# A decoder layer whose residual turns token-major, and whose MLP goes by slabs with seven half-size products

## The chip, the cores and the metric

The kernel runs on one core of a Trainium2 chip. Its engines work side by side, each through its own queue in order: TensorE multiplies matrices into PSUM banks, VectorE and ScalarE work element by element, GpSimd does a little of that too, and SyncE issues the DMAs that bring the weights. The metric is the device time of one launch in microseconds (us), the median of several runs.

## The reference

One decoder layer on 256 tokens, all in float32, with a residual stream of 2048 features, an MLP of 8192 hidden features and a per-layer embedding of 256:

```python
h = rmsnorm(x)
qA, kA, vA, qB, kB, vB, gA, gB = split(h @ w_in)
yA = dilated_mixture(qA, kA, vA)
yB = stick_breaking(qB, kB, vB)
x += (sigmoid(gA) * (yA @ w_branch_a) + sigmoid(gB) * (yB @ w_branch_b)) @ w_out
x += relu(rmsnorm(x) @ w_up) ** 2 @ w_down
x += (p @ w_ple_proj) * sigmoid(rmsnorm(x) @ w_ple_gate)
```

The change concerns what stands from `w_out` on: w_out is 2048x2048, w_up 2048x8192, w_down 8192x2048, w_ple_gate 2048x2048, w_ple_proj 256x2048.

## The kernel before, in words

**Two parts for each number.** TensorE's fast format (float32r) doesn't hold all of a float32. `split` makes of each operand a high part, a copy by ScalarE rounded to that format, and a low part, what is left, by VectorE. A product is then three: high by high, high by low and low by high. Activations have their two parts side by side in one tile (`[P, 4, 2, T]`: k tile, part, token). Weights come in chunks of 1 MB by SyncE (`load`, tiles `raw`), and each half chunk, 128 partitions by 1024 columns, is split into `wh` (ScalarE, L79) and `wl` (VectorE, L80). The pool `wts` has three buffers for each of raw, wh and wl; a buffer is free again when the matmuls that read it are done.

**Two shapes of product.** `group_t` gives feature-major results, 128 features on the partitions: the weight is the stationary operand, and for each k tile and each of two blocks of 128 features one matmul of 512 columns (L135: `wh` against the activation's both parts) and one of 256 (L136: `wl` against the high part) run. `halves` adds the two halves of the result. A chunk is eight k tiles of 256 weight columns, so 16 such pairs. `group_m` gives token-major results, 128 tokens on the partitions: the activation is stationary, and for each k tile and each block of 128 tokens three matmuls of 512 weight columns run (L150 to L152). Before the change only queries, keys and values use it, from `w_out` on all is feature-major.

**From w_out on.** `residual` adds each block of w_out's result to `x`, splits it times the gain as `h2`, and GpSimd collects the squares in `acc`; one matmul with ones (L178) sums these over the partitions. The norm comes in behind the product of up, as `rb` in L504. The MLP goes by four quarters of the hidden features: eight groups of up, whose results go through relu, square and split into `u`, then eight groups of down, each added to `x` by `residual`. The embedding's product is spread over the last quarter. The gate's groups end in `gate_out`.

**What sets the order.** Each engine's queue has the order that the framework's scheduler makes of the program text. `later` puts attention work, norms and embedding aside, and `advance` emits each when products of a given time have been emitted. PSUM has eight banks, four for the tag `mm` and four for `at`.

## Time and profile before

| | |
|---|---|
| median of 3 runs | 1494.01 us (1493.19 to 1505.6) |
| span of the profiled execution | 1494.2 us |
| mean granted TensorE clock | 0.998 of full |
| TensorE busy | 1480.9 us |
| VectorE busy | 1007.3 us |
| ScalarE busy | 783.1 us |
| moved by DMA | 277.10 MB |

The profile is one execution as the hardware recorded it. The span runs from its first instruction to its last, and no other time of that execution is given. Busy time is the time in which an engine had an instruction at work; TensorE's matmuls overlap, so how many it can do in a stretch is read from start to start. The granted clock is the share of full clock that the chip let TensorE have.

### The profile page before, as it was taken

What the parts mean: (1) busy time and instruction counts of PE and PEld (TensorE: products, weight loads), DVE (VectorE), ACT (ScalarE), POOL (GpSimd) and SP (SyncE); (2) the same over time, 40 slices, a digit from 0 to 9 for tenths busy, and PEclk for the clock granted to TensorE, in tenths of its full rate; (3) what the DMA queues carried; (4) which work ended last, traced back from release to release, by engine and by line L of the source; (5) the groups of instructions that cost most, each with busy time, mean ns of one, the idle gap of its engine ahead of it and who ended that gap; (6) DMA issues with size and microseconds to landing.
All of it is one profiled execution on the core that took longest, in us unless ns stands there. A gap on an engine that the chain in (4) does not pass through costs nothing.

```text
span 1494.2 us, 20920 instructions
## 1 busy us (share of the span) xinstructions
PE 1480.9 (99%) x8252; PEld 1285.3 (86%) x8252; DVE 1007.3 (67%) x1463; ACT 783.1 (52%) x1130; POOL 133.7 (9%) x137
## 2 busy tenths in 40 slices
PE   8999999999999999999999999999999999999998
PEld 6788888888888888888888888888888888888887
DVE  7875666466676667767766567656676567777776
ACT  6454554489845555555544445444454445555553
POOL 3432000000000000441000000000000000024200
PEclk9999999999999999999999999999999999999999
DMA  7455444544455555555555555555555555555563
GB/s 297 150 193 190 173 157 163 191 170 168 153 193 197 174 193 188 179 197 175 193 197 187 184 194 197 184 185 196 194 182 189 197 179 187 198 177 189 189 211 109
DMA packets 41281, 277.10 MB, mean 185 GB/s; under 512 B 4704, under 2 KB 7136, under 8 KB 8288
## 3 DMA queue, kind: packets, MB, share of 16 engines
q1 hardware_dynamic: 41040, 275.76, 52.3%
q8 instruction: 64, 1.05, 0.3%
q14 instruction: 33, 0.27, 0.1%
q10 hardware_dynamic: 144, 0.02, 0.0%
HBM read 273.67 MB, written 2.10 MB: 185 GB/s over the span
## 4 chain that ended last, share of the span: by engine, by line
PE 96%; DVE 2%; DMA 0%; ACT 0%; POOL 0%; issue 0%; SPq 0%; ACTq 0%; DVEq 0%; POOLq 0%
PE ps_mm L135 55%; PE ps_mm L136 28%; PE ps_mm L151 3%; PE ps_mm L152 3%; PE ps_mm L150 3%; DVE wl L80 1%; PE ps_at L135 0%; DMA x<-in_xt 0%; PE ps_at L319 0%; DVE h L83 0%; PE ps_mm L537 0%; PE ps_mm L539 0%; PE ps_mm L538 0%; PE ps_at L136 0%; PE ps_at L320 0%
## 5 line engine op out<-in xcount | busy, mean ns | idle before, releaser
L80 DVE TENSOR_TENSOR wl<-raw,wh 128x1024 fp32r<-128x1024 f32 (+1 forms) x518 | 636.2, 1229 | 361.6 <-ACT wh L79 355.2
L79 ACT ACTIVATE wh<-raw 128x1024 fp32r<-128x1024 f32 (+1 forms) x518 | 546.1, 1055 | 461.4 <-PE ps_mm L135 369.8
L135 PE MATMUL ps_mm<-h,wh 128*128 128x512 f32 x2016 | 712.3, 397 | 0.0
L136 PE MATMUL ps_mm<-h,wl 128*128 128x256 f32 x2016 | 564.7, 280 | 0.0
L135 PEld LDWEIGHTS ps_mm<-h,wh 128*128 128x128 f32 x2016 | 377.8, 187 | 87.0 <-ACT wh L79 0.3
L136 PEld LDWEIGHTS ps_mm<-h,wl 128*128 128x128 f32 x2016 | 380.8, 189 | 0.5
L135 PE MATMUL ps_mm<-u,wh 128*128 128x512 f32 x1024 | 356.9, 393 | 0.0
L136 PE MATMUL ps_mm<-u,wl 128*128 128x256 f32 x1024 | 286.9, 280 | 0.0
L135 PEld LDWEIGHTS ps_mm<-u,wh 128*128 128x128 f32 x1024 | 191.7, 187 | 43.6
L136 PEld LDWEIGHTS ps_mm<-u,wl 128*128 128x128 f32 x1024 | 193.5, 189 | 0.0
L161 ACT ACTIVATE ev<-ps_mm 128x256 f32<-128x256 f32 x158 | 59.7, 378 | 91.9 <-PE ps_mm L136 91.9
L150 PE MATMUL ps_mm<-wh,h 128*128 128x512 f32 x256 | 101.7, 400 | 2.6 <-ACT wh L79 2.6
L151 PE MATMUL ps_mm<-wl,h 128*128 128x512 f32 x256 | 101.5, 397 | 2.0 <-DVE wl L80 1.9
L454 POOL TENSOR_TENSOR acc<-x 128x256 f32<-128x256 f32 x2 | 3.3, 1653 | 1112.9 <-DVE x L449 1112.9
L152 PE MATMUL ps_mm<-wh,h 128*128 128x512 f32 x256 | 101.4, 396 | 0.0
L162 DVE TENSOR_TENSOR es<-ps_mm,ev 128x256 f32<-128x256 f32 x158 | 66.4, 421 | 44.2 <-ACT ev L161 44.0
L135 PE MATMUL ps_mm<-m,wh 128*128 128x512 f32 x256 | 90.5, 399 | 0.0
L136 PE MATMUL ps_mm<-m,wl 128*128 128x256 f32 x256 | 71.9, 281 | 0.0
L150 PEld LDWEIGHTS ps_mm<-wh,h 128*128 128x128 f32 x256 | 49.0, 192 | 14.8 <-ACT wh L79 4.9
L447 ACT ACTIVATE ev<-ps_mm 128x256 f32<-128x256 f32 x80 | 30.3, 379 | 59.0 <-PE ps_mm L136 59.0
L151 PEld LDWEIGHTS ps_mm<-wl,h 128*128 128x128 f32 x256 | 49.0, 191 | 13.8 <-DVE wl L80 3.8
L135 PEld LDWEIGHTS ps_mm<-m,wh 128*128 128x128 f32 x256 | 48.1, 188 | 12.1
(159 smaller groups left out, 1181.9 us busy)
## 6 DMA issues: line engine op xcount, KB each, us to landing
raw<-in_wup SPq DMA_DIRECT2D x64, 1024.0 KB, 4.7
raw<-in_wdn SPq DMA_DIRECT2D x64, 1024.0 KB, 4.8
raw<-in_wb SPq DMA_DIRECT2D x48, 1024.0 KB, 4.8
raw<-in_wa SPq DMA_DIRECT2D x31, 1024.0 KB, 4.8
raw<-in_wo SPq DMA_DIRECT2D x16, 1024.0 KB, 4.7
raw<-in_wpg SPq DMA_DIRECT2D x16, 1024.0 KB, 4.8
raw<-in_wba SPq DMA_DIRECT2D x8, 1024.0 KB, 4.7
raw<-in_wbb SPq DMA_DIRECT2D x8, 1024.0 KB, 4.7
```

The lines of the kernel that those rows point to most:

```text
L79: nc.scalar.activation(hi, src, AF.Copy)
L80: nc.vector.tensor_tensor(lo, src, hi.bitcast(F32), op=ALU.subtract)
L135: nc.tensor.matmul(ps[j], wh[:, c], flat(rhs[kt]), start=kt == 0, stop=False)
L136: nc.tensor.matmul(ps[j][:, :T], wl[:, c], rhs[kt][:, 0, :], start=False, stop=kt == last)
L150: nc.tensor.matmul(ps[tt], lhs[kt][:, 0, t], wh, start=kt == 0, stop=False)
L151: nc.tensor.matmul(ps[tt], lhs[kt][:, 0, t], wl, start=False, stop=False)
L152: nc.tensor.matmul(ps[tt], lhs[kt][:, 1, t], wh, start=False, stop=kt == last)
L161: nc.scalar.activation(t, ps[:, T:], AF.Copy)
L162: nc.vector.tensor_tensor(s, ps[:, :T], t, op=ALU.add)
L447: nc.scalar.activation(t, ps[:, T:], AF.Copy)
L454: nc.gpsimd.tensor_tensor(acc, xs(k), xs(k), op=ALU.mult)
```

## The change

Up to the end of the branches' merge (`m`) nothing changes but the pools. From `w_out` on:

- The residual stream is held token-major in two tiles `xr0` and `xr1` (128 tokens by 2048 features), loaded from a second copy of x, `xm`, 2 MB. w_out, w_down, the embedding and the gate become token-major products in the manner of `group_m`, and `add_rows` adds a bank of 512 columns to `xr`.
- The norm's squares are summed by ScalarE along each row (`squares_rows`), since a token is now a partition; `rows_norm` makes the reciprocal root. `turn` brings each finished piece of 512 columns feature-major, by transposes on TensorE into banks of the tag `at`, and splits it from there as h2 or h3.
- The norm before up isn't applied to up's result; its square, `r2`, scales down's result in `add_rows`.
- The MLP goes by eight slabs of 1024 hidden features. Slab 0's up stands alone; then `together` takes units of slab s's down and of slab s+1's up in turn. A unit of up is half a chunk (eight pairs), a unit of down a half chunk in `plain_units` (12 matmuls) or a whole product in `fast_units` (12 matmuls).
- For slabs 0 to 6, down's output columns 0 to 1023 are made by `fast_units`: the product of a 2x2 arrangement (two blocks of 128 tokens by two halves of 512 hidden features; these by two halves of 512 columns) in seven products of half size, not eight, 84 matmuls instead of 96. For it `hidden` makes four more planes by additions (tile `hr`), and the four quarters of the weight (tiles `quart`, 1 MB each) are added in place on VectorE. `keep` copies a bank between products (tile `cp`).
- Pools: `blk` has 6 buffers and `mblk` 9 in place of 15, `W1` is 7 instead of 8, and after w_out the mixers' pools are closed and `hid`, `mw` and `ps2` opened in their place. `ps2` has one bank each for x, z, w and y, two for `mm`, two for `at`.

The core of the diff:

```diff
+    def turn(g, h, gain, bank):
+        for half in range(2):
+            tp = bank("at")
+            for i in range(2):
+                k = 4 * g + 2 * half + i
+                for tt in range(2):
+                    o = (2 * i + tt) * P
+                    nc.tensor.transpose(tp[:, o:o + P], xr[tt][:, k * P:(k + 1) * P], ident)
+            for i in range(2):
+                k = 4 * g + 2 * half + i
+                split(h[k][:, 0, :], h[k][:, 1, :], tp[:, i * T:(i + 1) * T], gn[:, gain, k:k + 1])
...
+    for g in range(4):
+        ps = group_m([wo[g, c] for c in range(4)], m)
+        for tt in range(2):
+            add_rows(tt, g * PIECE, ps[tt])
+            squares_rows(tt, g, ss1, work.tile([P, PIECE], F32, tag="w2", name="junk", bufs=W2))
+        later(3, turn, g, h2, 1, bank)
...
+    def hidden(ps, fast):
+        n = 8 if fast else 4
+        s = mw.tile([P, 2, T], F32, tag="hs", name="hs", bufs=2)
         for j in range(2):
+            t = mw.tile([P, T], F32, tag="ev", name="ev", bufs=2)
+            nc.scalar.activation(t, ps[j][:, T:], AF.Copy)
+            nc.vector.tensor_tensor(s[:, j, :], ps[j][:, :T], t, op=ALU.add)
+        nc.scalar.activation(s, s, AF.Relu)
+        r = mw.tile([P, n, P], F32, tag="hr", name="hr", bufs=1)
+        nc.scalar.activation(r[:, 0:4, :].rearrange("p a t -> p (a t)"),
+                             s.rearrange("p a t -> p (a t)"), AF.Square)
+        if fast:
+            a21, a11, a22, a12 = (r[:, i, :] for i in range(4))
+            nc.vector.tensor_tensor(r[:, 4, :], a11, a21, op=ALU.subtract)
...
+        u = hid.tile([P, 2, n, P], F32R, tag="hid", name="u")
+        split(u[:, 0], u[:, 1], r)
+        return u
...
+    def up_units(s, out):
+        for g in range(4):
+            ps = [bank2("mm", 2) for _ in range(2)]
+            for c in range(2):
+                parts = weights(wup[4 * s + g, c], 8, 256)
...
+            out.append(hidden(ps, (s, 0) in FAST or (s, 1) in FAST))
+            yield
...
+        def product(ps, a, b, start):
+            for p0 in range(2):
+                for i, (wh, wl) in enumerate(split_weights(b[:, 2 * p0:2 * p0 + 2, :], 2, PIECE)):
+                    k = 2 * p0 + i
+                    nc.tensor.matmul(ps, f[k][:, 0, a, :], wh, start=start and k == 0, stop=False,
+                                     skip_group_check=not start)
+                    nc.tensor.matmul(ps, f[k][:, 0, a, :], wl, start=False, stop=False,
+                                     skip_group_check=not start)
+                    nc.tensor.matmul(ps, f[k][:, 1, a, :], wh, start=False, stop=k == 3,
+                                     skip_group_check=not start)
...
+        def add(a, b):
+            nc.vector.tensor_tensor(a, a, b, op=ALU.add)
...
+        product(px, A11, b[0, 0], True)
+        s1 = keep(px, 1)
+        add(b[0, 0], b[0, 1])
+        yield
+        product(pz, S1, b[0, 0], True)
+        z0 = keep(pz, 0)
+        add(b[0, 0], b[1, 1])
+        yield
+        product(px, S2, b[0, 0], False)
+        s2 = keep(px, 1)
+        add(b[0, 0], b[1, 0])
+        yield
+        product(pw, A22, b[0, 0], True)
+        w0 = keep(pw, 0)
+        add(b[0, 1], b[1, 1])
+        yield
+        product(py, A12, b[1, 0], True)
+        add(xr[1][:, left[0]], s1)
+        add_rows(1, c1, py, r2[:, 1:2])
+        yield
+        product(px, S3, b[0, 1], False)
...
+        product(pz, S4, b[1, 1], False)
```

The seven products are called P1 to P7 in this order below.

On VectorE, in the middle of a feature-major stage of the MLP before, the queue holds splits of weights (`wl`), the evacuation of up (`es`, `r2`) and its split (`u`):

```order
L80 TENSOR_TENSOR wl_7824<-raw_7821,wh_7823 128x1024
L80 TENSOR_TENSOR wl_7828<-raw_7821,wh_7827 128x1024
L162 TENSOR_TENSOR es_7802<-ps_mm_7715,ev_7801 128x256
L504 TENSOR_TENSOR es_7802<-es_7802,rb1_6193 128x256
L506 SCALAR_TENSOR_TENSOR r2_7806<-es_7802 128x256
L80 TENSOR_TENSOR wl_7866<-raw_7863,wh_7865 128x1024
L80 TENSOR_TENSOR u1_0_7711<-r2_7806,u1_0_7711 128x256
L162 TENSOR_TENSOR es_7811<-ps_mm_7716,ev_7810 128x256
L504 TENSOR_TENSOR es_7811<-es_7811,rb1_6193 128x256
```

On VectorE after the change, from the first split of P1's weight (`wl_7119`) of one slab on; `raw` belongs to up, `quart` to down, `hr` and `u` to the hidden features, L595 is `add`:

```order
L83 TENSOR_TENSOR wl_7129<-quart_7106,wh_7128 128x1024
L595 TENSOR_TENSOR quart_7106<-quart_7106,quart_7108 128x2048
L535 TENSOR_TENSOR hs_7089<-ps_mm_6955,ev_7090 128x256
L535 TENSOR_TENSOR hs_7089<-ps_mm_6956,ev_7093 128x256
L83 TENSOR_TENSOR wl_7146<-raw_7143,wh_7145 128x1024
L83 TENSOR_TENSOR wl_7150<-raw_7143,wh_7149 128x1024
L542 TENSOR_TENSOR hr_7097<-hr_7097 128x128
L543 TENSOR_TENSOR hr_7097<-hr_7097 128x128
L595 TENSOR_TENSOR quart_7108<-quart_7108,quart_7110 128x2048
L544 TENSOR_TENSOR hr_7097<-hr_7097 128x128
L83 TENSOR_TENSOR wl_7186<-quart_7106,wh_7185 128x1024
L545 TENSOR_TENSOR hr_7097<-hr_7097 128x128
```

The additions of weight quarters stand between the splits of up (`wl_7146`, `wl_7150`) and those of the next product (`wl_7186`). Some rows on it goes on so, to the last split of P7's weight, `wl_7440`:

```order
L83 TENSOR_TENSOR wl_7196<-quart_7106,wh_7195 128x1024
L83 TENSOR_TENSOR u_7103<-hr_7097,u_7103 128x1024
L595 TENSOR_TENSOR quart_7106<-quart_7106,quart_7110 128x2048
L83 TENSOR_TENSOR wl_7211<-raw_7208,wh_7210 128x1024
L83 TENSOR_TENSOR wl_7215<-raw_7208,wh_7214 128x1024
L83 TENSOR_TENSOR wl_7235<-quart_7106,wh_7234 128x1024
L595 TENSOR_TENSOR xr1_5282<-xr1_5282,cp_7138 128x512
L595 TENSOR_TENSOR xr0_5281<-xr0_5281,cp_7205 128x512
L83 TENSOR_TENSOR wl_7245<-quart_7106,wh_7244 128x1024
L595 TENSOR_TENSOR quart_7106<-quart_7106,quart_7112 128x2048
```

The split of the hidden block `u_7103` and that of the next up half chunk, `wl_7211`, each stand behind an addition of 128x2048.

On TensorE at the joint of w_out and the MLP before, the norm's product (L178) stands among up's pairs, some way into the first group:

```order
L135 MATMUL ps_mm<-h_3_5279,wh 128x512
L136 MATMUL ps_mm<-h_3_5279,wl 128x256
L178 MATMUL ps_at<-acc,cs 128x256
L135 MATMUL ps_mm<-h_3_5279,wh 128x512
L136 MATMUL ps_mm<-h_3_5279,wl 128x256
L135 MATMUL ps_mm<-h_3_5279,wh 128x512
```

On TensorE at the same joint after the change, from w_out's last matmuls (L153 to L155) over the last `turn` (L476) to up's first pair:

```order
L154 MATMUL ps_mm_5759<-wl_5887,m3_4000 128x512
L155 MATMUL ps_mm_5759<-wh_5886,m3_4000 128x512
L476 MATMUL ps_at_5920<-idt_82,xr0_5281 128x128
L476 MATMUL ps_at_5929<-idt_82,xr0_5281 128x128
L476 MATMUL ps_at_5920<-idt_82,xr1_5282 128x128
L476 MATMUL ps_at_5920<-idt_82,xr0_5281 128x128
L476 MATMUL ps_at_5920<-idt_82,xr1_5282 128x128
L476 MATMUL ps_at_5929<-idt_82,xr1_5282 128x128
L476 MATMUL ps_at_5929<-idt_82,xr0_5281 128x128
L476 MATMUL ps_at_5929<-idt_82,xr1_5282 128x128
L562 MATMUL ps_mm_5966<-h2_0_5285,wh_5970 128x512
L563 MATMUL ps_mm_5966<-h2_0_5285,wl_5971 128x256
```

The transposes of w_out's last piece now stand between w_out and up, where before no instruction of TensorE needed that piece for long.

## Rows read from the trace of the kernel before

**Rows 1.** Page: busy time of two engines; the chain that ended last, by engine.

```profile
PE 1480.9 (99%) x8252; PEld 1285.3 (86%) x8252; DVE 1007.3 (67%) x1463; ACT 783.1 (52%) x1130; POOL 133.7 (9%) x137
PE 96%; DVE 2%; DMA 0%; ACT 0%; POOL 0%; issue 0%; SPq 0%; ACTq 0%; DVEq 0%; POOLq 0%
```

**Rows 2.** Page, costliest groups: busy and mean ns, idle before and its releaser.

```profile
L80 DVE TENSOR_TENSOR wl<-raw,wh 128x1024 fp32r<-128x1024 f32 (+1 forms) x518 | 636.2, 1229 | 361.6 <-ACT wh L79 355.2
L79 ACT ACTIVATE wh<-raw 128x1024 fp32r<-128x1024 f32 (+1 forms) x518 | 546.1, 1055 | 461.4 <-PE ps_mm L135 369.8
```

**Rows 3.** Waits of TensorE: us in total, times, longest.

```profile
PE ps_at L288 <- POOL qn L282: 2.6, 1, 2.6
PE ps_mm L150 <- ACT wh L79: 2.6, 2, 1.5
PE ps_mm L151 <- DVE wl L80: 1.9, 2, 1.4
...
```

**Rows 4.** Timeline of TensorE, 900 to 908 us: start, duration, instruction.

```profile
900.18 0.39 PE L135 MATMUL ps_mm<-h,wh 128*128 128x512 f32 x1
...
907.46 0.39 PE L135 MATMUL ps_mm<-h,wh 128*128 128x512 f32 x1
```

**Rows 5.** Timeline of TensorE, 85 to 90 us, token-major.

```profile
86.23 0.40 PE L151 MATMUL ps_mm<-wl,h 128*128 128x512 f32 x1
...
89.86 0.39 PE L152 MATMUL ps_mm<-wh,h 128*128 128x512 f32 x1
```

**Rows 6.** Chain of waits in order of time: start, duration, transposes and norm product.

```profile
85.28 0.87 PE ps_at L288 x8
...
683.41 0.43 PE ps_at L178 x2
```

**Rows 7.** Groups by line and shape, whole kernel: busy, mean ns, idle before.

```profile
L162 DVE TENSOR_TENSOR es<-ps_mm,ev 128x256 f32<-128x256 f32 x158 | 66.4, 421 | 44.2 <-ACT ev L161 44.0
L161 ACT ACTIVATE ev<-ps_mm 128x256 f32<-128x256 f32 x158 | 59.7, 378 | 91.9 <-PE ps_mm L136 91.9
...
L83 DVE SCALAR_TENSOR_TENSOR h<-x,gn,h 128x256 fp32r<-128x256 f32 x48 | 37.0, 787 | 2.5 <-ACT h L82 2.4
...
L82 ACT ACTIVATE h<-x,gn 128x256 fp32r<-128x256 f32 x48 | 23.3, 506 | 2.4 <-DMA gn<-in_gains 0.8 <-DMA x<-in_xt 0.4
...
L360 ACT ACT_TABLE_LOAD x8 | 10.3, 1283 | 0.1
...
L273 DVE TENSOR_TENSOR qn<-qraw,qr 128x512 f32<-128x512 f32 x8 | 5.5, 693 | 0.4
...
L265 ACT ACTIVATE qraw<-ps_mm,rt 128x512 f32<-128x512 f32 x8 | 5.4, 676 | 3.1 <-PE ps_mm L152 3.1
...
L239 ACT ACTIVATE q<-x 128x512 f32<-128x512 f32 x8 | 4.6, 615 | 0.0
...
L335 ACT ACTIVATION_READ_ACCUMULATOR e<-z,st 128x1 f32 x16 | 3.0, 187 | 0.0
```

**Rows 8.** Windows: busy of PE, PEld, DVE, ACT, POOL; granted clock; DMA share; GB/s.

```profile
23.00:25.00 2.00, 2.00 (x10) 1.59 (x10) 2.00 (x2) 0.58 (x1) 1.87 (x2) 1.00 0.32 135
...
63.00:64.00 1.00, 1.00 (x4) 0.73 (x3) 0.87 (x4) 0.00 (x0) 0.00 (x0) 0.50 0.00 0
```

**Rows 9.** Timeline of TensorE at the two waits; idle time before in brackets.

```profile
22.73 0.50 PE L151 MATMUL ps_mm<-wl,h 128*128 128x512 f32 x1 [1.38 <-DVE wl L80]
...
61.20 0.66 PE L288 MATMUL ps_at<-cs,qn 128*128 128x128 f32 x4 [2.63 <-POOL qn L282]
```

**Rows 10.** Timeline of VectorE, 900 to 903 us: a split and the next instruction.

```profile
900.97 1.22 DVE L80 TENSOR_TENSOR wl<-raw,wh 128x1024 fp32r<-128x1024 f32 x1
902.11 0.42 DVE L80 TENSOR_TENSOR u<-r,u 128x256 fp32r<-128x256 f32 x1
```

**Rows 11.** Timeline of the end: the first and the last step behind the last product.

```profile
1489.68 0.42 DVE L522 TENSOR_TENSOR g<-ps_mm,rb 128x256 f32<-128x256 f32 x1 [0.42 <-PE ps_mm L539]
...
1491.11 0.42 DVE L525 TENSOR_TENSOR o<-o,x 128x256 f32<-128x256 f32 x1
```

More of the change, by code (lines that the diff above doesn't have):

```diff
@@ L183, in norm_rows @@
         return rb
-    x = [block([P, 8, T], F32, f"x{i}") for i in range(2)]
+    x = [block([P, 8, T], F32, f"x{i}", blk) for i in range(2)]
     gn = const.tile([P, 3, DT], F32, name="gn")
@@ L532, in layer_kernel @@
-    parts = [weights(wpg[7, c], 8, 256) for c in range(2)]
-    for j in range(2):
-        ps = bank("mm")[:, :T]
-        c = slice(j * P, (j + 1) * P)
-        for kt, (wh, wl) in enumerate(parts[0] + parts[1]):
-            nc.tensor.matmul(ps, wh[:, c], h3[kt][:, 0, :], start=kt == 0, stop=False)
-            nc.tensor.matmul(ps, wh[:, c], h3[kt][:, 1, :], start=False, stop=False)
-            nc.tensor.matmul(ps, wl[:, c], h3[kt][:, 0, :], start=False, stop=kt == DT - 1)
-        gate_out(14 + j, ps)
+    xr = [block([P, D], F32, f"xr{tt}", blk) for tt in range(2)]
@@ new lines, in layer_kernel @@
+    h2 = new_acts("h2_", pool=blk)
+    ss1 = const.tile([P, 2, 4], F32, name="ss1")
+    for g in range(4):
+        ps = group_m([wo[g, c] for c in range(4)], m)
+        for tt in range(2):
+            add_rows(tt, g * PIECE, ps[tt])
+            squares_rows(tt, g, ss1, work.tile([P, PIECE], F32, tag="w2", name="junk", bufs=W2))
+        later(3, turn, g, h2, 1, bank)
+    rms = []
+    later(6, lambda: rms.append(rows_norm(ss1, "rt1", work)))
+    advance(0)
+    while pending:
+        advance(1.0)
@@ new lines, in layer_kernel, with bank2 @@
+    mixers.close()
+    mlp = ExitStack()
+    hid = mlp.enter_context(tc.tile_pool(name="hid", bufs=7))
+    mw = mlp.enter_context(tc.tile_pool(name="mw", bufs=2))
+    ps2 = mlp.enter_context(tc.tile_pool(name="ps2", bufs=1, space=PSUM))
+    FAST = [(s, 0) for s in range(7)]
+    def bank2(tag, bufs=1):
+        return ps2.tile([P, 512], F32, tag=tag, name=f"ps_{tag}", bufs=bufs)
+    r2 = const.tile([P, 2], F32, name="r2")
+    r2n = const.tile([P, 1], F32, name="r2n")
+    nc.vector.tensor_tensor(r2, rms[0], rms[0], op=ALU.mult)
@@ new lines, in plain_units @@
+    def plain_units(s, n, u):
+        for j in range(2):
+            ps = [bank2("x" if tt else "z") for tt in range(2)]
+            for i in range(2):
+                raw = load(wdn[s, n, i, j], 4, PIECE)
+                for k, (wh, wl) in enumerate(split_weights(raw, 4, PIECE)):
+                    for tt in range(2):
+                        a = 2 * i + tt
+                        last = i == 1 and k == 3
+                        nc.tensor.matmul(ps[tt], u[k][:, 0, a, :], wh, start=i + k == 0, stop=False)
+                        nc.tensor.matmul(ps[tt], u[k][:, 0, a, :], wl, start=False, stop=False)
+                        nc.tensor.matmul(ps[tt], u[k][:, 1, a, :], wh, start=False, stop=last)
+                    advance(1.36)
+                    if k == 1:
+                        yield
+                if i == 0:
+                    yield
+            for tt in range(2):
+                add_rows(tt, (2 * n + j) * PIECE, ps[tt], r2[:, tt:tt + 1])
+            yield
@@ new lines, in down_units, with together @@
+    def down_units(s, u, done=None):
+        for n in range(2):
+            if (s, n) in FAST:
+                yield from fast_units(s, n, u)
+            else:
+                yield from plain_units(s, n, u)
+            if done is not None:
+                done(2 * n)
+                done(2 * n + 1)
+    def together(a, na, b, nb):
+        ia = ib = 0
+        for _ in range(na + nb):
+            if ia * nb <= ib * na and ia < na or ib >= nb:
+                next(a, None)
+                ia += 1
+            else:
+                next(b, None)
+                ib += 1
+        for x_ in (a, b):
+            for _ in x_:
+                pass
@@ new lines, in layer_kernel, with finished @@
+    ss2 = const.tile([P, 2, 4], F32, name="ss2")
+    h3 = []
+    def finished(g):
+        if g == 0:
+            h3.extend(new_acts("h3_", pool=blk))
+        for tt in range(2):
+            squares_rows(tt, g, ss2, mw.tile([P, PIECE], F32, tag="cp", name="junk", bufs=5))
+        later(3, turn, g, h3, 2, lambda tag: bank2("at", 2))
+    hids = [[]]
+    for _ in up_units(0, hids[0]):
+        pass
+    for s in range(8):
+        hids.append([])
+        if s < 7:
+            b, nb = up_units(s + 1, hids[s + 1]), 16
+        else:
+            b, nb = embedding_units(), 4
+        na = sum(7 if (s, n) in FAST else 8 for n in range(2))
+        together(down_units(s, hids[s], finished if s == 7 else None), na, b, nb)
@@ L593 @@
             for n, a in arrays.items()]
[L594 removed]
+    out = nc.dram_tensor("out", (2, P, D), F32, kind="ExternalOutput").ap()
     with tile.TileContext(nc) as tc:
```

229 lines of the change are left out of this document (138 added, 91 removed).

## The prediction, as it was written before the result

> **What bounds the kernel now.** I read the page's busy times and its chain first: TensorE is busy 99% of 1494.2 us, the chain of work that ended last is 96% TensorE and 2% VectorE, VectorE is busy 67% [rows 1]. So a product that is left out is worth its slot, as long as the next operand is there. Then the two rows of the split of a weight, which show who waits for whom: ScalarE makes `wh` and is idle 461 us, mostly for TensorE to free a buffer; VectorE makes `wl` and is idle 362 us, nearly all of it for `wh` [rows 2]. The splits run ahead as far as three buffers allow and then wait; TensorE waits for a split for only 2.6 and 1.9 us in the whole kernel [rows 3]. That lead over TensorE is the cover on which the change leans, so the question is what VectorE has left in each stage, not its 67%.
>
> The execution that was profiled has a span of 1494.2 us; the median of the three runs is 1494.01, so I sum against 1494.2. A measurement of this kernel tells about 1% (15 us) from no change.
>
> **What leaves TensorE and what comes.** A feature-major pair (512 and 256 columns) takes 0.3466 us from start to start (900.18 to 907.46 is 21 pairs) [rows 4]; a token-major matmul of 512 columns takes 0.227 (86.23 to 89.86 is 16) [rows 5]. Three of these do the work of two pairs: 0.681 against 0.693. w_down: 1024 pairs, 354.9 us, become 7 x (84 + 96) + 192 = 1452 matmuls, 329.6 us: -25.3. w_out: 256 pairs (88.7) become 384 matmuls (87.2): -1.5. The gate: 224 pairs and the last group's products (77.6 + 11.5) become 87.2: -1.9. Embedding -0.2. The two norm products of the kernel before (0.43 each, about 0.5 with their slot) go: -1.1. 64 transposes come at 0.11 (eight in 0.87 us) [rows 6]: +7.0. **Sum -23.0 us.** Up is unchanged. The 2 MB of `xm` and the embedding's other layout cost TensorE nothing: the loads that hide them have landed long before.
>
> **The joint between w_out and the MLP.** Before, `residual` turns out h2 feature by feature and the first up product needs only its k tile 0, long done. After the change the last two 512-column pieces must be added to `xr`, transposed, and split, and the first up product takes over the bank that the last transposes fill; it waits until the last h2 split has read it, on VectorE behind: two adds from PSUM (0.69 each), and on ScalarE behind two squares (0.6 each), their accumulator reads (0.19 each) and, between the splits, a table load of 1.28 for the root, then four splits of 128x256 at 0.51 on ScalarE and 0.79 on VectorE [rows 7]. Worked along the order: the adds end 1.6 after the last product, the transposes 2.5, the first two splits at about 3.9, the table load holds ScalarE until 5.2, the last two splits end at 7.3, and with the handover TensorE goes on at 7.5 instead of 0.9: **+6.6**. The ends are 4.5 (the root drifts behind the splits) and 8. [...]
>
> **Slab 0's up stands alone.** In `up_units` the four banks of before are two, so at each of three group ends the next group's first product waits for `hidden` to read both banks: ScalarE 0.38, VectorE 0.42 [rows 7] with handovers about 0.8: **+2.4**. In the later slabs a unit of down lies between.
>
> **The stage with seven products.** From the end of one slab's plain units to the next plain unit, TensorE has 84 matmuls (19.1) and nine half chunks of up (9 x 8 x 0.3466 = 24.9): 44.0 us. VectorE's rows from `wl_7119` to `wl_7440` are what these need. A split of 128x1024 takes 1.22 and the next op starts 1.14 after it [rows 10]: 24 x 1.14 = 27.4. Four adds of 128x2048 on the quarter weights have no row: 128x512 takes 0.69 and 128x1024 1.23 [rows 2, 7], so 1.05 ns an element more, 2.3 at 2048, 2.2 in succession: 8.9. Nine adds on `xr` (0.61): 5.5. Four `hs` (0.34): 1.4. Eight adds in `hr` (128x128, by the same slope 0.28, 0.2 in succession): 1.6. Together **44.8 us for 44.0 of TensorE**, where one feature-major chunk before asks 2.3 in 5.5. [...]
>
> Lower end: VectorE can begin 1.4 us before the stage, since its buffers are still being read, and must be through 3.4 before its end, so at least 44.8 - 1.4 + 3.4 - 44.0 = 2.8, or 20 us in seven slabs. But order costs more: a product's half split feeds TensorE for six matmuls, 1.36 us, where a split in plain or up feeds 2.7, and each add stands in front of splits that TensorE needs sooner. Walked along the two orders with these spacings, an ACT to VectorE handover of 0.03 and 0.2 from a matmul's slot: (1) the first half chunk of up is wanted at 5.3, but `wl_7146` stands behind the add of `quart_7106`, 2.2, and two `hs`, and comes at 6.7: 1.4 lost. (2) P1's last k needs the hidden block `u_7103`, and the next half chunk `wl_7211`, both behind the adds of `quart_7108` and of `quart_7106`: 16.2 wanted, 18.7 had, together with the 0.5 before it 3.0 lost. (3) P4's first split stands behind the third add on `quart_7106` and behind an `xr` add that needs P3: 1.4. Scraps 0.7. **6.5 us a slab, 45.5 in seven.** The upper end adds, at P5, P6 and P7, a wait of VectorE for the product that an `xr` add reads, 0.8 each with the add itself in front of the next split: 9 us a slab, 63. I take the walk: its durations are rows of before. The plain half is free of this: 15 splits of weights, two of `u`, and few small ops ask 25 us of VectorE for 41.2 of TensorE (96 x 0.227 + 56 x 0.3466).
>
> **The end.** Slab 7's two finished pieces go through squares, transposes and splits before the gate; most is under embedding and plain units, the last piece is not: +2 (0 to 6, as at the first joint). Before, the last product is followed by 0.42 us steps on 128x256, from 1489.68 to 1491.53 [rows 11]; now two pieces of 128x512 share VectorE, 0.3 + 0.68 (L265 [rows 7]) + 4 x 0.65 = 3.6 against 2.16: about +1.5.
>
> **Sum:** 1494.2 - 23.0 + 6.6 + 1.6 + 2.4 + 45.5 + 2 + 1.5 = 1530.8; I forecast **1530**.
>
> **The rivals.** *A, the forecast: VectorE paces the seven-product stage in its order.* Own range 1512 to 1548, chance 0.55.
>
> *B, the cover holds.* The adds and splits fall into VectorE's idle time (362 us of it [rows 2]), the joint costs 6.6 and 1.6, the rest 4: 1494.2 - 23 + 8.2 + 4 = 1483; with the joint at its low end, 1478. For it: in stages like the plain half VectorE has 16 us to spare. Against: `wts` holds three buffers, so that can't be saved up for the stage that follows, and there 44.8 stands beside 44.0. This ends faster than before, from the point where the stage's wait is under 1.9 us a slab. Chance 0.11: 0.08 of it under 1479.
>
> *C, the clock falls in the stage.* The waits at (2) join into one near 3 us, like the 2.63 that left the clock at 0.50 [rows 8, 9]; one or two such falls a slab at 1.6 each add 11 to 22 us: 1542 to 1553. For: the size of (2). Against: the 1.38 at 22.7 left it at 1.00, and (1) and (3) are of that size. [...] The trace before has one fall, after the longest pause in it. Chance 0.14.
>
> *D, only the bound counts.* VectorE is never late but by the 2.8 a slab that it lacks: 1494.2 - 23 + 8.2 + 2.4 + 20 + 3.5 = 1505; with a shorter joint 1500. Within 1% of before. For: the 45.5 rests on a walk through orders that shifts wherever a wait elsewhere shifts. Against: in-order queues, with three adds in front of urgent splits. Chance 0.20.
>
> **How the numbers follow.** Faster by over 1% (under 1479): 0.08, from B. Within 1% (1479 to 1509): the rest of B 0.03, D 0.18, the low end of A 0.03: 0.24. Slower: 0.68. The range takes A, C's most and D's upper half: 1498 to 1549; outside it lie B and the tails, 0.18.
>
> **What would show it.** TensorE's busy time should fall to about 1460 while its waits, 7 us before but for the start [rows 3], rise to some 60, in the seven-product stages above all, with VectorE's `wl` on weights and `quart` as releaser; there VectorE should be busy 95% or more, in the plain half some 60. Right after w_out one gap of 5 to 7 us with a granted clock near 0.5 behind it; no such gap of that length elsewhere. If VectorE shows pauses in the seven-product stage while TensorE is never late, B is right; if its splits there take longer than 1.23, the walk is too kind; if TensorE waits but for another releaser (a DMA on `quart`, ScalarE's `wh`), the time may fit and the reason be wrong. I'd be wrong in size if the order lets splits pass ahead of the adds.

## The result and the profile after

The change makes the kernel slower: 1539.43 us in the median of four runs against 1495.22, a ratio on record of 1.0257 with a 95% interval of 1.0211 to 1.0303. (The quotient of these two medians is 1.0296; executions of the kernel before fall into two groups, 1493 to 1497 and 1500 to 1508 us, here three and one, and the 1494.2 of its profile belongs to the lower.) The forecast was 1530. The profiled execution has a span of 1537.9 us.

The page's busy times and the chain of the kernel after answer to [rows 1]:

```profile
PE 1483.5 (96%) x7412; PEld 1236.3 (80%) x7412; DVE 1068.1 (69%) x1366; ACT 860.1 (56%) x1153; POOL 57.7 (4%) x75
...
PE 86%; DVE 8%; ACT 3%; issue 1%; DMA 0%; POOL 0%; SPq 0%; DVEq 0%; ACTq 0%; POOLq 0%
```

TensorE issues 840 matmuls fewer and is busy no less; a tenth of the chain has gone over to VectorE and ScalarE. Its waits, against [rows 3] (L563 is up's low part, L583 a product's, L562 up's high part):

```profile
PE ps_mm L563 <- DVE wl L83: 20.0, 14, 2.2
PE ps_w L583 <- DVE wl L83: 5.3, 7, 0.8
PE ps_mm L562 <- DVE rs L492: 4.3, 1, 4.3
PE ps_mm L562 <- DVE hs L535: 3.5, 10, 0.6
PE ps_mm L154 <- DVE wl L83: 2.8, 3, 1.4
PE ps_at L293 <- POOL qn L287: 2.7, 1, 2.7
PE ps_x L581 <- ACT u L82: 2.6, 7, 0.4
```

The counts of 7 and 14 say where they are: once or twice in each of the seven slabs with products P1 to P7. TensorE's timeline in the second of these slabs shows all of them; the brackets hold the idle time and its releaser:

```profile
825.63 0.73 PE L562 MATMUL ps_mm<-h,wh 128*128 128x512 f32 x2 [0.25 <-DVE hs L535]
827.00 0.50 PE L563 MATMUL ps_mm<-h,wl 128*128 128x256 f32 x2 [0.64 <-DVE wl L83]
834.35 0.50 PE L581 MATMUL ps_x<-wh,u 128*128 128x512 f32 x1 [0.37 <-ACT u L82]
839.13 0.50 PE L563 MATMUL ps_mm<-h,wl 128*128 128x256 f32 x2 [2.22 <-DVE wl L83]
847.48 0.51 PE L581 MATMUL ps_w<-wh,u 128*128 128x512 f32 x1 [0.17 <-ACT wh L82]
848.74 0.51 PE L583 MATMUL ps_w<-wl,u 128*128 128x512 f32 x1 [0.76 <-DVE wl L83]
```

These are three places: up's first half chunk, P1's last step with the next half chunk, and P4. The brackets add up to 4.4 us; from start to start, which counts that the first matmul behind a wait also takes longer (0.50 and 0.51 us in the rows of P1 and P4, 0.39 to 0.40 in those without a wait), 1.4, 3.1 and 1.5, in all 6.0. VectorE's timeline over the same stretch shows what stood ahead of the splits:

```profile
822.86 2.29 DVE L595 TENSOR_TENSOR quart<-quart 128x2048 f32<-128x2048 f32 x1
825.07 0.75 DVE L535 TENSOR_TENSOR hs<-ps_mm,ev 128x256 f32<-128x256 f32 x2
825.73 2.35 DVE L83 TENSOR_TENSOR wl<-raw,wh 128x1024 fp32r<-128x1024 f32 x2
...
833.38 1.23 DVE L83 TENSOR_TENSOR wl<-quart,wh 128x1024 fp32r<-128x1024 f32 x1 [1.15 <-ACT wh L82]
834.52 1.22 DVE L83 TENSOR_TENSOR u<-hr,u 128x1024 fp32r<-128x1024 f32 x1
835.66 2.28 DVE L595 TENSOR_TENSOR quart<-quart 128x2048 f32<-128x2048 f32 x1
837.86 2.35 DVE L83 TENSOR_TENSOR wl<-raw,wh 128x1024 fp32r<-128x1024 f32 x2
```

The split that TensorE needs at 836.9 starts at 837.86, behind an addition of 2.28. But at 833.38 VectorE has been idle for 1.15 us, waiting for ScalarE: a queue that is late and idle in turn. The windows of the kernel after (busy of PE, PEld, DVE, ACT, POOL; granted clock; DMA share; GB/s) give this slab's stage from P1's first matmul to P7's last, the rest of the slab, and two us behind the longest wait in the first and in the second slab:

```profile
823.12:869.05 45.93, 41.52 (x203) 33.04 (x201) 42.07 (x46) 29.39 (x35) 0.00 (x0) 1.00 0.45 161
869.05:915.85 46.80, 46.80 (x237) 39.42 (x236) 30.92 (x38) 23.48 (x28) 0.00 (x0) 1.00 0.57 202
745.50:747.50 2.00, 2.00 (x8) 1.71 (x7) 2.00 (x3) 0.00 (x0) 0.00 (x0) 0.50 0.31 53
839.60:841.60 2.00, 2.00 (x14) 1.75 (x13) 2.00 (x3) 0.05 (x1) 0.00 (x0) 1.00 0.19 33
```

VectorE is busy 92% of the stage, not all of it. A slab takes 92.7 us where its products ask 85.2.

At the joint behind w_out, TensorE's timeline of the kernel after:

```profile
674.64 0.88 PE L476 MATMUL ps_at<-idt,xr 128*128 128x128 f32 x6 [0.16 <-DVE xr L459]
679.83 0.76 PE L562 MATMUL ps_mm<-h,wh 128*128 128x512 f32 x1 [4.32 <-DVE rs L492]
```

and the window behind it, with the clock at 0.50:

```profile
680.00:683.00 3.00, 3.00 (x10) 2.52 (x11) 0.30 (x2) 0.00 (x0) 0.00 (x0) 0.50 0.69 191
```

### The profile page after: what moved, and what is told of

It is laid out like the page before. It is cut to its first block, busy times and chain, and to the rows that moved or that the text cites. A ratio compares the mean times of both kernels' runs of the same rounds, so it can differ in the third digit from the quotient of the medians.

```text
span 1537.9 us, 19021 instructions
## 1 busy us (share of the span) xinstructions
PE 1483.5 (96%) x7412; PEld 1236.3 (80%) x7412; DVE 1068.1 (69%) x1366; ACT 860.1 (56%) x1153; POOL 57.7 (4%) x75
## 4 chain that ended last, share of the span: by engine, by line
PE 86%; DVE 8%; ACT 3%; issue 1%; DMA 0%; POOL 0%; SPq 0%; DVEq 0%; ACTq 0%; POOLq 0%
PE ps_mm L138 16%; PE ps_mm L562 14%; PE ps_mm L139 8%; PE ps_mm L563 7%; PE ps_mm L154 5%; PE ps_mm L155 5%; PE ps_mm L153 5%; DVE wl L83 4%; DVE quart L595 3%; ACT wh L82 2%; PE ps_z L645 2%; PE ps_z L647 2%; PE ps_x L645 2%; PE ps_z L646 2%; PE ps_x L647 2%; PE ps_x L646 2%
## 5 line engine op out<-in xcount | busy, mean ns | idle before, releaser
L83 DVE TENSOR_TENSOR wl<-raw,wh 128x1024 fp32r<-128x1024 f32 (+1 forms) x462 | 566.7, 1232 | 346.3 <-ACT wh L82 342.3
L82 ACT ACTIVATE wh<-raw 128x1024 fp32r<-128x1024 f32 (+1 forms) x462 | 486.4, 1054 | 372.0 <-PE ps_mm L155 112.8
L562 PE MATMUL ps_mm<-h,wh 128*128 128x512 f32 x1024 | 370.6, 402 | 7.8 <-DVE rs L492 4.3
L563 PE MATMUL ps_mm<-h,wl 128*128 128x256 f32 x1024 | 287.0, 284 | 20.0 <-DVE wl L83 20.0
L138 PE MATMUL ps_mm<-h,wh 128*128 128x512 f32 x768 | 276.8, 403 | 0.0
L562 PEld LDWEIGHTS ps_mm<-h,wh 128*128 128x128 f32 x1024 | 194.6, 190 | 56.1 <-issue 9.1
L563 PEld LDWEIGHTS ps_mm<-h,wl 128*128 128x128 f32 x1024 | 194.5, 191 | 30.4 <-DVE wl L83 25.1
L139 PE MATMUL ps_mm<-h,wl 128*128 128x256 f32 x768 | 215.4, 280 | 0.0
L82 ACT ACTIVATE wh<-quart 128x1024 fp32r<-128x1024 f32 x98 | 103.8, 1059 | 92.7 <-PE ps_mm L562 70.0
L83 DVE TENSOR_TENSOR wl<-quart,wh 128x1024 fp32r<-128x1024 f32 x98 | 119.6, 1221 | 34.2 <-ACT wh L82 33.0
L153 PE MATMUL ps_mm<-wh,h 128*128 128x512 f32 x256 | 101.4, 399 | 2.4 <-ACT wh L82 2.4
L155 PE MATMUL ps_mm<-wh,h 128*128 128x512 f32 x256 | 100.8, 394 | 0.0
L595 DVE TENSOR_TENSOR quart<-quart 128x2048 f32<-128x2048 f32 x28 | 64.1, 2288 | 0.5
L153 PEld LDWEIGHTS ps_mm<-wh,h 128*128 128x128 f32 x256 | 48.7, 191 | 14.8 <-ACT wh L82 4.8
L645 PE MATMUL ps_z<-wh,u 128*128 128x512 f32 x144 | 57.6, 400 | 2.3 <-ACT u L82 1.3
L155 PEld LDWEIGHTS ps_mm<-wh,h 128*128 128x128 f32 x256 | 48.8, 191 | 10.1
L647 PE MATMUL ps_z<-wh,u 128*128 128x512 f32 x144 | 56.8, 394 | 0.0
L645 PE MATMUL ps_x<-wh,u 128*128 128x512 f32 x144 | 56.8, 394 | 0.0
```

The costliest lines, as they stand in the source:

```text
L82: nc.scalar.activation(hi, src, AF.Copy)
L83: nc.vector.tensor_tensor(lo, src, hi.bitcast(F32), op=ALU.subtract)
L138: nc.tensor.matmul(ps[j], wh[:, c], flat(rhs[kt]), start=kt == 0, stop=False)
L139: nc.tensor.matmul(ps[j][:, :T], wl[:, c], rhs[kt][:, 0, :], start=False, stop=kt == last)
L153: nc.tensor.matmul(ps[tt], lhs[kt][:, 0, t], wh, start=kt == 0, stop=False)
L155: nc.tensor.matmul(ps[tt], lhs[kt][:, 1, t], wh, start=False, stop=kt == last)
```

## The experiments

They ran on three chips, and each ratio is to the kernel before on the same chip, whose medians there were 1503.87 to 1506.05 us; the changed kernel's ratio is 1.0257. Times compare as they are, too: up to w_out's first product only the pools differ, and the traces of these runs reach it at 581.7 to 584.2 us, the changed kernel's at 583.8 and that of before at 583.6. A slab's period is from P1's first matmul to the next slab's (down's first, where there are no products).

**The additions left out.**

```diff
-        add(b[0, 0], b[0, 1])
...
-        add(b[0, 0], b[1, 1])
...
-        add(b[0, 0], b[1, 0])
...
-        add(b[0, 1], b[1, 1])
```

> The four additions of weight quarters on VectorE are left out in each of the seven slabs, so that all seven products take the loaded quarters as they are; nothing else changes. Theory (VectorE paces the seven-product stage): VectorE is asked 35.9 us there instead of 44.8, TensorE 44.0 as now. The waits of 0.64 and 2.2 us for up's split and of 0.76 for the fourth product's split go but for scraps, no clock falls in the slabs: a slab period goes from 92.8 to about 86, the time from 1539 to 1488 to 1496. Rival (the half-size products themselves are the cause: a half split feeds only 1.36 us of TensorE, so three buffers are too short a lead whatever VectorE has left): the waits stay at more than half, above 1515.

Measured: 1505.08 us, ratio 1.0017 (0.9992 to 1.0042). The window of its stage, as above:

```profile
817.02:858.60 41.58, 41.20 (x203) 33.21 (x201) 34.18 (x42) 29.50 (x35) 0.00 (x0) 1.00 0.52 181
```

The slab is 88.4 instead of 92.7, the rest of it 46.80 as before; no clock falls there. So the additions cost 4.35 us a slab, 30 in all, and 4 more by the clock. The expectation still missed: the period stays above its 86, and the time is 9 us above its range. What is left over the 85.2 is 1.3 to 1.4 of longer slots (see the end) and 1.7 around waits, of which the profile shows this one, once in each of the seven slabs:

```profile
PE ps_z L583 <- DVE wl L83: 2.6, 7, 0.4
```

So a part of the waits, though the smaller one, comes without any addition in the queue.

**No seven products.**

```diff
-    FAST = [(s, 0) for s in range(7)]
+    FAST = []
```

> No slab uses the seven products: both halves of down's columns by plain units in all eight slabs, with no additions in hr and none on the weights; the token-major residual, the slabs and the pools stay. Theory: 84 matmuls of 0.227 us come back, +19.1, and the slabs lose all their waits, about 53, and three clock falls, 4; the joint behind w_out (7.4 us with its clock), slab 0's group ends (2.3) and the end stay: 1539 + 19 - 57 = about 1501, within 1498 to 1506. Rival (the turns of up and down, not the seven products, make the waits): above 1520.

Measured: 1511.26 us, ratio 1.0072 (1.0048 to 1.0096): far below its rival, but 5 us above the range. Slabs take 89.5, without a wait inside, where their products ask 88.0; these longer slots, some 11 us in seven slabs, stay, where the expectation let 53 us go. So even with no addition at all the seven products were 1.1 us a slab better than eight, not the 2.7 of twelve matmuls.

**One PSUM pool.**

```diff
-    psum = mixers.enter_context(tc.tile_pool(name="psum", bufs=4, space=PSUM))
+    psum = ctx.enter_context(tc.tile_pool(name="psum", bufs=4, space=PSUM))
...
-        return ps2.tile([P, 512], F32, tag=tag, name=f"ps_{tag}", bufs=bufs)
+        return psum.tile([P, 512], F32, tag="mm" if tag in "xzwy" else "at", name=f"ps_{tag}")
```

> One PSUM pool stays open from start to end, with its four banks mm for down and gate and its four banks at for up, transposes and embedding; all sums and their order in the text stay. Theory (the joint is a wait for a bank that the last transposes' splits hold): up's first product no longer waits, the gap of 4.3 us and the clock at 0.5 behind it go, 5.4 + 2.0; up's groups have four banks in turn, so slab 0's three group ends lose 0.75 each (2.3), and in the seven slabs the 0.4 before the first product of an up group goes or is swallowed by the next wait (0 to 3). 1539 - 10 to 13 = 1526 to 1530. Rival (TensorE would meet at the joint the norm's or the splits' own delay, so the gap only moves): 1535 or more.

Measured: 1526.45 us, ratio 1.0172 (1.0131 to 1.0214), 0.85% or 13 us better. TensorE's timeline at its joint:

```profile
673.24 0.39 PE L155 MATMUL ps_mm<-wh,m 128*128 128x512 f32 x1
673.92 0.44 PE L476 MATMUL ps_at<-idt,xr 128*128 128x128 f32 x2 [0.29 <-DVE xr L459]
674.11 0.48 PE L561 MATMUL ps_mm<-h,wh 128*128 128x512 f32 x1
```

Up begins at 674.11 instead of 679.83, at full clock. The seven slabs keep 92.8 to 94.1: the 0.25 us for `hs` that goes there is taken up by the next wait for `wl`. Whether the wait was for the bank itself or for the closing of the old pool isn't told apart by this run.

**The fourth addition later.**

```diff
-        add(b[0, 1], b[1, 1])
+        with tc.issue_after(getattr(lows[0], 'ins', lows[0])):
+            add(b[0, 1], b[1, 1])
```

> Only VectorE's order in the seven-product stage changes: the addition of the two quarters for the sixth product is queued behind the last split of the fourth product instead of ahead of the second's; VectorE's work is the same. Theory (order within a VectorE that is full): the hidden block's split and up's next split come 2.2 us sooner, so the wait of 2.2 shrinks to some 0.5, its clock falls go; the waits of 0.64 and 0.76 stay; later in the stage the addition may cost up to 1 us anew. Per slab 92.8 goes to 90.5 to 91.5: 1539 - 9 to 16 - 4 = 1519 to 1526. Rival (only VectorE's sum counts, not its order): the wait goes elsewhere and the time stays within 1533 to 1541.

Measured: 1548.3 us, ratio 1.0317 (1.0274 to 1.0359): no gain, rather a loss. The long wait has gone from its place and come back at P4 and P5. Waits of TensorE in this run:

```profile
PE ps_w L583 <- ACT wh L84: 11.1, 7, 1.6
PE ps_y L583 <- ACT wh L84: 7.9, 7, 1.3
PE ps_w L585 <- DVE wl L85: 5.3, 7, 0.8
PE ps_mm L565 <- DVE wl L85: 4.4, 7, 0.6
```

The scheduler also put the second addition behind another split of up, and ScalarE's copy for P3 now waits 1.08 us for it; how the delay runs on from there to P4 and P5 isn't worked out here. The time is even above what its rival gave: the clock falls in five slabs instead of three.

**Products spread over the slab.** In `down_units`, on top of one PSUM pool; the plain units of these slabs also take their banks from the tag `at`, which up uses:

```diff
+        if (s, 0) in FAST:
+            a, b = fast_units(s, 0, u), plain_units(s, 1, u)
+            for _ in range(7):
+                next(a)
+                yield
+                next(b)
+                yield
```

> One PSUM pool as in the earlier run with it, and in each of the seven slabs the seven products alternate with the eight plain units instead of standing ahead of them; every instruction's work stays. Theory (VectorE has enough time in a slab, 70 of 85 us, but not in the stage where the products stand in a row): with the additions and half splits spread over the slab its demand is 82% everywhere, most waits for its splits go; what stays is the start of a slab, where two additions, up's evacuation and a hidden block meet (1 to 2 us). Slab period 87 to 88.5 instead of 93, no clock falls in the slabs; ratio to the kernel before 0.985 to 0.997. Rival (each product waits for its own short split wherever it stands): period above 91, ratio above 1.006.

Measured: 1533.68 us, ratio 1.0196 (1.0165 to 1.0226). The expectation fell: slabs take 93.4 to 95.0, no better than in a row, though VectorE is busy 77% of a slab and about evenly over it (35.6 and 36.4 us in the halves of the one from 907.69). VectorE's timeline in one slab shows why:

```profile
926.48 1.22 DVE L83 TENSOR_TENSOR wl<-quart,wh 128x1024 fp32r<-128x1024 f32 x1 [1.91 <-ACT wh L82]
930.34 1.23 DVE L83 TENSOR_TENSOR wl<-quart,wh 128x1024 fp32r<-128x1024 f32 x1 [2.63 <-ACT wh L82]
931.48 0.42 DVE L534 TENSOR_TENSOR hs<-ps_mm,ev 128x256 f32<-128x256 f32 x1
931.81 2.28 DVE L594 TENSOR_TENSOR quart<-quart 128x2048 f32<-128x2048 f32 x1
934.01 0.42 DVE L534 TENSOR_TENSOR hs<-ps_mm,ev 128x256 f32<-128x256 f32 x1
```

and ScalarE's of the same time:

```profile
929.24 1.06 ACT L82 ACTIVATE wh<-quart 128x1024 fp32r<-128x1024 f32 x1 [2.79 <-PE ps_z L584]
```

VectorE idles 2.63 us for ScalarE, which waits for TensorE to free a buffer, and then puts 2.28 us of addition ahead of the `hs` that TensorE is waiting for by then (1.21 at 934.49). Of the 7.0 us that this slab loses by waits, that one is 1.4, and a part of it may be owed to the banks that up shares here; the other 5.6 are waits for splits. So time to spare didn't help a queue that may only be three splits ahead. From here on the theory was: long operations in a short lead.

**Spread, and the fourth addition later**: both steps above.

> As e5_spread, and the addition for the sixth product is queued on VectorE behind the last split of the fourth product's weight. Theory: spread, VectorE has room there, so unlike in the crowded stage, where the same step only moved the wait to the next products' ScalarE copies, it takes 1 to 2 us from the slab's start and gives nothing back: 0.5 to 1.5 us a slab less than e5_spread, ratio 0.980 to 0.993. Rival (order doesn't matter, or the addition is late for the sixth product): equal to e5_spread within 0.3% or above it.

Measured: 1539.49 us, ratio 1.0236 (1.0204 to 1.0268). The wait moved again, to P3 and P5 (`wh`, 0.7 in each of seven slabs each) and up; its expectation fell with the one before it.

**No seven products, one pool.** The two edits shown above together.

> One PSUM pool, and no slab with the seven products: what the token-major residual and the slabs give alone, without the joint's wait. Theory: the run without seven products stood at 1.0072 of before; minus the joint with its clock (7.4 us) and slab 0's group ends (2.3): 1.0005 to 1.002. TensorE's own count would be 1494.2 - 23 + 19.1 = 1490 with 1.5 us of longer slots in each slab, 11, and some 1.3 at the end, so no gain over before. Rival (the joint's delay comes back behind the norm): 1.006 or more.

Measured: 1500.49 us, ratio 0.9969 (0.9955 to 0.9983), a little better than expected. So the token-major residual and the slabs alone give 0.3% by the ratio, once the joint is mended; but its runs, 1498.5 to 1500.93, all lie above the fastest of before on the same chip, 1495.74, so this is not a gain to count on.

**The fourth addition on GpSimd**, on top of the spread order:

```diff
-        add(b[0, 1], b[1, 1])
+        nc.gpsimd.tensor_tensor(b[0, 1], b[0, 1], b[1, 1], op=ALU.add)
```

> As e5_spread, with the addition for the sixth product on GpSimd in place of VectorE. Theory: 2.2 us a slab leave VectorE; GpSimd, which took 2.08 us for 128x512, takes about 8 for it and has time until the sixth product; as good as e6_spread_late_add or 0.2 to 0.5 us a slab better: ratio 0.978 to 0.993. Rival (GpSimd and VectorE slow each other in memory, and VectorE's splits get longer than 1.23): VectorE's mean split above 1.27 and the time above e5_spread.

Measured: 1557.66 us, ratio 1.0356 (1.0325 to 1.0386): the rival. The addition on GpSimd, in its timeline, and the two splits of VectorE that start at 819.1 and 824.2, in the view of the tile (min, median, max ns):

```profile
818.68 4.52 POOL L617 TENSOR_TENSOR quart<-quart 128x2048 f32<-128x2048 f32 x1 [92.37 <-DVE quart L594]
```

```profile
L83 DVE TENSOR_TENSOR wl<-raw,wh x2: 1211/3179/5147, 819.1 to 824.2; 128x1024 fp32r<-128x1024 f32 x2
```

The first of the two takes 5.15 us instead of 1.22, so it is longer by 3.9, nearly all of the 4.1 us that it shares with GpSimd's 4.52. In the other six slabs the same split takes 5.2 to 5.3. TensorE then waits 5.2 us once a slab. That the two slow each other in memory, as the rival has it, isn't shown: the run shows the longer split beside GpSimd's addition, not its cause.

**Additions in halves**, one pool, products in a row:

```diff
         def add(a, b):
-            nc.vector.tensor_tensor(a, a, b, op=ALU.add)
+            for c in ((slice(0, 2), slice(2, 4)) if len(a.shape) == 3 else (slice(None),)):
+                nc.vector.tensor_tensor(a[:, c], a[:, c], b[:, c], op=ALU.add)
```

> One PSUM pool, seven products in a row as in the changed kernel, and each addition of weight quarters made as two of 128x1024 in place of one of 128x2048: the same elements, 2.28 us of VectorE for 2.22. Theory after the runs with spread products (not VectorE's sum but one long operation in a short lead: three buffers let the splits be 1.4 to 5.5 us ahead, and an addition of 2.2 in front of one eats that): the halves let a split pass in between and the next product start on its first half, so of the 6.2 us of waits a slab 2 to 3 go: period 89.5 to 91 instead of 92.9, ratio 0.998 to 1.011. Rival (VectorE's sum in the stage): no less than 92.5, ratio 1.015 or more.

Measured: 1508.23 us, ratio 1.0049 (1.0025 to 1.0072). Slabs take 90.5, the first 91.8, and no clock falls in them any more. The same elements on the same engine cost 2.4 us a slab less. Two things change by the cut, and the run doesn't tell them apart: another operation can stand between two halves, and a product's copy and split can start on the first half.

**Four buffers** for the parts of weights in the MLP, one pool, additions whole. The room for them comes from the hidden block, kept and split in two tiles of 128x512 instead of one of 128x1024, and from one buffer less of `hs` and of `cp`; so that split of VectorE's is cut in two as well, and the run doesn't tell this from the fourth buffer:

```diff
-            wh = wts.tile([P, n, cols], F32R, tag="wh", name="wh")
-            wl = wts.tile([P, n, cols], F32R, tag="wl", name="wl")
+            turns[0] += 1
+            pool = wts if not extra or turns[0] % 4 else extra[0]
+            wh = pool.tile([P, n, cols], F32R, tag="wh", name="wh", bufs=3 if pool is wts else 1)
+            wl = pool.tile([P, n, cols], F32R, tag="wl", name="wl", bufs=3 if pool is wts else 1)
```

> One PSUM pool, seven products in a row, additions whole, and from the MLP on four buffers each for the high and the low parts of weights instead of three; the memory comes from the hidden tile's planes kept in two tiles (its split in two operations), one buffer less of hs and of cp. Theory (short lead): one more buffer is 1.4 us of TensorE in the seven products and 2.8 in up, so the wait of 2.2 goes to 0.5 or less and those of 0.64 and 0.76 go: period 88.5 to 90.5, ratio 0.996 to 1.009. Rival (order and sum alone, the lead doesn't matter since VectorE is never idle there): above 92, ratio above 1.014.

Measured: 1511.6 us, ratio 1.0066 (1.0045 to 1.0087), inside the range but not evenly: from the second slab on, slabs take 88.35 and 92.8 in turn. Windows of the stage in two neighbours:

```profile
810.79:852.57 41.78, 40.50 (x204) 33.59 (x203) 40.85 (x49) 29.09 (x37) 0.00 (x0) 1.00 0.51 183
899.14:944.40 45.26, 41.60 (x199) 33.96 (x197) 41.83 (x48) 29.57 (x37) 0.00 (x0) 0.96 0.47 168
```

In the longer ones TensorE waits 2.67 us for P4's `wh`, a wait that the longer lead doesn't cover, and the clock falls behind it.

**Up and down in blocks**, no seven products, one pool:

```diff
+        if s < 7:
+            for _ in b:
+                pass
+            for _ in down_units(s, hids[s]):
+                pass
```

> One PSUM pool, no seven products, and the whole of up of slab s+1 ahead of the whole of down of slab s, not in turn; TensorE's matmuls are the same. In the runs with turns each matmul of the seven slabs took 1.1 to 1.5% longer from start to start than in stretches of one kind, without a wait that the profile names: 1.5 us a slab. Theory (the turns of up and down cause that): the slots go back to 0.2269 and 0.3467, a slab takes 88.0 instead of 89.5, time 10 us below the run with turns: ratio 0.989 to 0.992. Rival (it comes from the operands' new places in memory): a slab stays at 89.5, ratio 0.996 to 0.998.

Measured: 1493.02 us, ratio 0.9946 (0.9924 to 0.9968). A slab takes 88.8, between the theories: down's matmuls go back from 0.232 to 0.2270, up's pairs do not. TensorE's timeline of this run, 16 pairs of up apart, 0.354 each:

```profile
830.18 0.40 PE L561 MATMUL ps_mm<-h,wh 128*128 128x512 f32 x1
...
835.84 0.40 PE L561 MATMUL ps_mm<-h,wh 128*128 128x512 f32 x1
```

**Halves and four buffers**, with the seven products, one pool:

> Both steps that worked, with the seven products: the additions of weight quarters in two halves, and four buffers for the parts of weights (with them the hidden tile in two, one buffer less of hs and of cp), in one PSUM pool. With halves alone a slab takes 90.45, with four buffers alone 88.35 in three slabs and 92.8 in three. Theory (long operations in a short lead): together no wait over 0.7 us is left in any slab, no clock falls there, a slab takes 87 to 88.4 (85.2 of products, 1.1 of longer slots, the rest scraps), the time 1487 to 1498 on a before of 1494, ratio 0.989 to 0.999; then the seven products are worth 1 to 2 us a slab against plain units in turn (89.5), not the 2.7 of their left-out matmuls. Rival (the additions' sum still shows): a slab at 89.5 or more, ratio above 1.001.

Measured: 1486.91 us against 1504.56, ratio 0.9891 (0.9861 to 0.9921): faster than both kernels, with all six runs (1484.88 to 1487.69) below the fastest of before on record, 1493.19. Windows of a slab, stage and rest:

```profile
810.80:851.46 40.66, 40.65 (x206) 33.99 (x205) 39.86 (x50) 29.54 (x37) 0.00 (x0) 1.00 0.51 181
851.46:897.73 46.27, 46.27 (x235) 38.93 (x234) 32.78 (x41) 23.79 (x30) 0.00 (x0) 1.00 0.56 205
```

VectorE is busy 98% of the stage, more than in the changed kernel, and TensorE has no gap. Behind w_out this run still waits 2.11 us for a `wh`, with the clock at half behind it. The slab's 86.9 is 2.6 below the plain one in turns: here twelve left-out matmuls are worth twelve matmuls.

## Why the prediction was right, and where its reason was not

The direction and the walk held; what failed is the step that called the cause VectorE's sum, and two terms that were missing from the sum.

| term | forecast | measured | from |
|---|---|---|---|
| TensorE's work | -23.0 | about -28 | longer slots of before, in w_out and its last quarter, see the end |
| joint | 6.6 + 1.6 | 5.4 + 2.0 | gap and the slots at half clock behind it |
| slab 0 alone | 2.4 | 2.3 | three waits of 0.63, 0.58, 0.58 and their restarts |
| waits with seven products | 45.5 | 42 to 43 | 6.0 to 6.1 in each of seven slabs |
| clock falls there | 0 | 4.0 | three slabs of 94.0 to 94.3 among those of 92.7 to 93.0 |
| longer slots in the slabs | 0 | 9.5 | 1.3 to 1.4 us in each of seven |
| slab 7 and gate | 2 | 2.8 | waits of 1.32, 0.45 and 0.50 |
| end | 1.5 | 1.3 | last product at 1531.74, span 1537.9; before 1489.37 and 1494.2 |

1494.2 and the column come to about 1536; the span is 1537.9. The rest is in steps too small to name. No run shows the 1.6 us which the sum puts down for the clock behind the joint, and rival C for each of its falls, an estimate of the author's: the kernel after had 0.50 of full clock in 680 to 683, where the slots took 2.0 us longer, and lost some 1.3 by the clock in each of three slabs. That the forecast came so near is in part luck: 5 us of work and 3 of waits less than forecast stand against 13.5 of longer slots and clock that it had put at nothing.

**The walk.** "6.5 us a slab" was 6.0 to 6.1, at the three places named: (1) 1.4, measured 1.4; (2) 3.0, 3.1; (3) 1.4, 1.5. The durations of before carried over: the addition of 128x2048 had been put at 2.3 from two rows and took 2.288, the splits 1.23 and 1.22.

**The step that failed: the bound of 2.8 a slab, made from "44.8 us for 44.0 of TensorE".** The sum was about right, but it did not set the time. The windows from P1's first split to P7's last in the second slab, in the kernel after and in the last run:

```profile
818.70:867.73 49.03, 44.62 (x219) 35.75 (x217) 45.79 (x49) 29.64 (x36) 0.00 (x0) 1.00 0.47 170
...
803.69:849.60 45.91, 45.90 (x233) 38.52 (x232) 45.16 (x55) 30.75 (x38) 0.00 (x0) 1.00 0.46 163
```

VectorE has as much to do in the last run, 45.2 us against 45.8, and TensorE waits for none of it; in the kernel after VectorE itself is idle for 3.2 us of this stretch. The spread run has VectorE busy 77% of a slab, and TensorE loses 7.0 us there. What set the time, by the runs, was an operation of 2.2 us in an in-order queue whose lead over TensorE is three buffers. In a row and at full clock a slab takes 92.8 with the additions whole, 90.5 with them halved, 88.35 without them; with four buffers it takes 88.35 in every second slab, and with both steps 86.9. So the additions cost 4.4 of these 5.9 us, and 1.5 stay without any of them; the longer lead or the finer operations of the last run took these away too. What a slab would take at three buffers if only VectorE's sum counted, no run shows: with the halves alone 3.5 us over the last run remain. The prediction's other sentence, that an addition stands in front of splits that TensorE needs sooner, was the main cause. Its last one, that it would be off "if the order lets splits pass ahead", names a part of the remedy: of the halves those of the first addition let a split pass, while those of the second still stand together ahead of up's split, and TensorE's wait there is 1.44 instead of 2.22.

**Rival C** took a part, 4 of its 11 to 22 us: three falls, not seven. **D**, the bound, fell as a forecast with the step above. **B** came true only in the last run, once the cover had been made longer and the additions shorter; its reason, VectorE's idle time, was not enough, as the spread run shows. B's 1478 and D's 1500 take 5 us off the joint, where its low end of 4.5 without a fall of the clock takes off 3.7; no chance hangs on that.

**What was missing.** From the first slab in turns on, matmuls came further apart than the rows from which they were costed, without a named wait. And the pair of 0.3466 was read at 900 us, but in w_out and in the last quarter of before a pair takes 0.353, so the change took away some 5 us more there than the -23.0 counts.

**The forecast's signs.** All rows of TensorE's waits, of which seven stand above, sum to 48.5 us, where "some 60" had been written. Its busy time did not fall to 1460, since slots at half clock and longer slots count as busy: 1483.5. VectorE was busy 92%, not 95, in the stage, and 66% in the rest (some 60 forecast). The gap behind w_out was 4.3 with the clock at 0.50 behind it.

## What to carry to other kernels

Before work is saved on the engine that bounds, ask of each operation that it puts on another queue how long it is beside the lead that the buffers allow: here an addition of 2.28 us ahead of a split cost TensorE 2.22 us at one place, and spreading the work did not mend that: with VectorE busy 77% of a slab, TensorE still lost 7.0 us of it. Cut such operations to the grain of their consumers and lengthen the lead (86.9 us a slab with both, 92.7 without); moving one to a later place in the same queue only moved the wait (1548.3 us against 1539.43). At a joint where a pool is closed and another opened, look for whom the first product of the new stage waits (4.32 us here).
